# 2x2 average pooling: two result buffers in loop bodies of two tiles, and the wait for the last stores in a section of its own

## Chip, cores, metric

One core of a Trainium2 chip. The metric is the device time of one execution in microseconds (us), as the median of repeated runs.

## The reference

```python
x: (32, 128, 256, 256) float32, kernel_size 2, stride 2
for i in range(128):
    for j in range(128):
        window = x[:, :, 2*i:2*i+2, 2*j:2*j+2]
        output[:, :, i, j] = np.mean(window, axis=(2, 3))
```

1073.7 MB are read and 268.4 MB written; each output is the mean of four inputs.

## The kernel before

Two input rows lie side by side in memory and make one output row, so the work is 524288 rows of 512 floats in and 128 out. A tile is 32 such rows on each of 128 partitions: a load of 8.4 MB (64 KB per partition) and a store of 2.1 MB (16 KB per partition). 127 whole tiles are followed by one that is split into parts of 16, 8, 4 and 4 rows. SyncE (SP) issues loads into two input buffers, VectorE (DVE) adds twice, ScalarE (ACT) scales by 0.25 and issues the store. All waits are written by hand; `take` waits for a semaphore and takes the count off again.

```python
OUTS = 4                                   # result buffers
def tile_sum(b, o, first=False):           # DVE
    it, dst = ins[b], res[o]
    take(dve, loaded[b], 16)
    dve.tensor_add(out=it[:, :, 0:w], in0=it[:, :, 0:w], in1=it[:, :, w:]).then_inc(ready)
    if not first:
        take(dve, stored[o], 16)           # result buffer is free: ahead of the SECOND add
    take(dve, ready)
    dve.tensor_add(out=dst, in0=it[:, :, 0:w:2], in1=it[:, :, 1:w:2]).then_inc(summed)
def tile_scale(b, o, done):                # ACT
    take(act, summed)
    act.sem_inc(free[b])                   # SP may load this input buffer again
    act.mul(out=res[o], in_=res[o], mul=0.25).then_inc(done)
def tile_store(t, o):
    take(act, scaled)
    act.dma_start(out=ot[t], in_=res[o]).then_inc(stored[o], 16)
...                                        # loop bodies of four tiles on DVE and ACT, two on SP
with tc.tile_critical():
    ...
    take(sp, tail, 16 * len(parts))        # the end: four waits, in the one critical section
    for o in range(OUTS):
        if o != whole % OUTS:
            take(sp, stored[o], 16)
```

Of the kernel before, what the change touches and what calls it, by code (L numbers as in the profile page):

```python
# [9 lines left out]
@with_exitstack  # L10
def kernel(
    ctx: ExitStack,
    tc: tile.TileContext,
    x: bass.AP,
    kernel_size: bass.AP,
    stride: bass.AP,
    out: bass.AP,
):
    nc = tc.nc
    P = nc.NUM_PARTITIONS  # L20

    n, c, h, w = x.shape
    k = int(kernel_size)
    s = int(stride)
    h_out = (h - k) // s + 1
    w_out = (w - k) // s + 1
    R = n * c * h_out
    units = R // P if R % P == 0 else 0


    if k == 2 and s == 2 and h % 2 == 0 and w == 256 and units >= 1024:
        _pool_2x2(ctx, tc, x, out, units)
    else:
        _generic_pool(ctx, tc, x, out, k, s, n, c, h, w, h_out, w_out)


TILE = 32
OUTS = 4


def _pool_2x2(ctx, tc, x, out, units):
    nc = tc.nc
    P = nc.NUM_PARTITIONS
    f32 = mybir.dt.float32
    w = x.shape[3]
    w_out = w // 2
    sp, act, dve = nc.sync, nc.scalar, nc.vector

    xv = x.rearrange("n c (ho a) w -> (n c ho) (a w)", a=2)
    ov = out.rearrange("n c ho wo -> (n c ho) wo")  # L50

    in_pool = ctx.enter_context(tc.tile_pool(name="inp", bufs=2))
    out_pool = ctx.enter_context(tc.tile_pool(name="outp", bufs=OUTS))
    ins = [in_pool.tile([P, TILE, 2 * w], f32, name="in_tile") for _ in range(2)]
    res = [out_pool.tile([P, TILE, w_out], f32, name="res") for _ in range(OUTS)]

    loaded = [ctx.enter_context(nc.semaphore(f"loaded{b}")) for b in range(2)]
    free = [ctx.enter_context(nc.semaphore(f"free{b}")) for b in range(2)]
    summed = ctx.enter_context(nc.semaphore("summed"))
    scaled = ctx.enter_context(nc.semaphore("scaled"))  # L60
    stored = [ctx.enter_context(nc.semaphore(f"stored{b}")) for b in range(OUTS)]
    tail = ctx.enter_context(nc.semaphore("tail"))
    ready = ctx.enter_context(nc.semaphore("ready"))
    held = ctx.enter_context(nc.semaphore("held"))



    def take(engine, sem, n=1):
        engine.wait_ge(sem, n)
        engine.sem_inc(sem, -n)  # L70

    def block(r0, g):
        rows = slice(r0, r0 + g * P)
        return xv[rows].rearrange("(p g) f -> p g f", p=P), ov[rows].rearrange("(p g) f -> p g f", p=P)

    whole, rest = divmod(units - 1, TILE)
    rest += 1
    xt = xv[0:whole * TILE * P].rearrange("(t p g) f -> t p g f", p=P, g=TILE)
    ot = ov[0:whole * TILE * P].rearrange("(t p g) f -> t p g f", p=P, g=TILE)
    loops, left = divmod(whole - OUTS, OUTS)  # L80

    def tile_load(t, b):
        sp.dma_start(out=ins[b], in_=xt[t]).then_inc(loaded[b], 16)

    def tile_sum(b, o, first=False):
        it, dst = ins[b], res[o]
        take(dve, loaded[b], 16)
        dve.tensor_add(out=it[:, :, 0:w], in0=it[:, :, 0:w], in1=it[:, :, w:]).then_inc(ready)  # L88
        if not first:
            take(dve, stored[o], 16)  # L90
        take(dve, ready)
        dve.tensor_add(out=dst, in0=it[:, :, 0:w:2], in1=it[:, :, 1:w:2]).then_inc(summed)  # L92

    def tile_scale(b, o, done):
        take(act, summed)
        act.sem_inc(free[b])
        act.mul(out=res[o], in_=res[o], mul=0.25).then_inc(done)  # L97

    def tile_store(t, o):
        take(act, scaled)  # L100
        act.dma_start(out=ot[t], in_=res[o]).then_inc(stored[o], 16)

    parts, a = [], 0
    while a < rest:
        b = rest if rest - a <= 4 else a + (rest - a) // 2
        parts.append((a, b))
        a = b

    psem = [ctx.enter_context(nc.semaphore(f"part{k}")) for k in range(len(parts))]

    with tc.tile_critical():

        for b in range(2):
            tile_load(b, b)
        with sp.Fori(2, 2 + 2 * ((whole - 2) // 2), 2) as i:
            for b in range(2):
                take(sp, free[b])
                tile_load(i + b, b)
        t = 2 + 2 * ((whole - 2) // 2)
        while t < whole:  # L120
            take(sp, free[t % 2])
            tile_load(t, t % 2)
            t += 1



        take(sp, free[whole % 2])
        it, dst = ins[whole % 2], res[whole % OUTS]
        for (a, b), s in zip(parts, psem):
            sp.dma_start(out=it[:, a:b], in_=block((whole * TILE + a) * P, b - a)[0]).then_inc(s, 16)  # L130
        take(sp, held)
        sp.dma_start(out=ot[whole - 1], in_=res[(whole - 1) % OUTS]).then_inc(stored[(whole - 1) % OUTS], 16)


        for o in range(OUTS):
            tile_sum(o % 2, o, first=True)
        with dve.Fori(0, loops) as i:
            for o in range(OUTS):
                tile_sum(o % 2, o)
        for o in range(left):  # L140
            tile_sum(o % 2, o)
        take(dve, stored[whole % OUTS], 16)
        for (a, b), s in zip(parts, psem):
            take(dve, s, 16)
            dve.tensor_add(out=it[:, a:b, 0:w], in0=it[:, a:b, 0:w], in1=it[:, a:b, w:]).then_inc(ready)  # L145
            take(dve, ready)
            dve.tensor_add(out=dst[:, a:b], in0=it[:, a:b, 0:w:2], in1=it[:, a:b, 1:w:2]).then_inc(summed)  # L147


        for t in range(OUTS):  # L150
            tile_scale(t % 2, t, scaled)
            tile_store(t, t)
        with act.Fori(OUTS, OUTS + loops * OUTS, OUTS) as i:
            for o in range(OUTS):
                tile_scale(o % 2, o, scaled)
                tile_store(i + o, o)
        for t in range(OUTS + loops * OUTS, whole):
            tile_scale(t % 2, t % OUTS, scaled if t < whole - 1 else held)
            if t < whole - 1:
                tile_store(t, t % OUTS)  # L160
        act.sem_inc(free[(whole + 1) % 2], -1)
        for a, b in parts:
            take(act, summed)
            act.mul(out=dst[:, a:b], in_=dst[:, a:b], mul=0.25).then_inc(scaled)  # L164
            take(act, scaled)
            act.dma_start(out=block((whole * TILE + a) * P, b - a)[1], in_=dst[:, a:b]).then_inc(tail, 16)


        take(sp, tail, 16 * len(parts))
        for o in range(OUTS):  # L170
            if o != whole % OUTS:
                take(sp, stored[o], 16)


def _generic_pool(ctx, tc, x, out, k, s, n, c, h, w, h_out, w_out):
# [92 lines left out]
```

## Time and profile before

| what | value | from |
|---|---|---|
| time | 3103.83 us (3103.81 to 3103.89, 3 runs) | result |
| span of the profiled run | 3103.1 us | page, first line |
| DVE, ACT busy | 54%, 15% | page, part 1 |
| DMA engines | full in all 40 slices, 433 GB/s | page, part 2 |
| period of a tile | 24.18 us | timeline |
| issue to landing, median | store 33.9, load 34.6 us | page, part 6 |

The page's lines are printed in the prediction. They are read from the resource that has no time left: the DMA row. The wait lists of the page's engines lead only to the line of `take`, and its chain only to the last activation, not to the transfers.

One more view of before is needed for the end of the program: the instructions of the line that holds `take`, and those of the line that opens the critical section, in the last 3 us (columns: line, engine, operation, count; duration in ns; first and last start in us).

```profile
L70 SPq EVENT_SEMAPHORE  x4: 17/17/17, 3101.8 to 3102.0; - x4
L111 SPq NOP  x1: 13/13/13, 3102.3 to 3102.3; - x1
```

Four waits stand one after another behind the last landing, and then SyncE leaves the section it shares with ACT and DVE.

### The profile page before, as it was taken

The numbers are of one execution on the slowest core, as the hardware profiler recorded it, in microseconds if no ns is written. First come the engines' busy times: TensorE is split into PE (matmuls) and PEld (weight loads), VectorE is DVE, ScalarE is ACT, GpSimd is POOL, SyncE is SP. The second block draws the span as 40 slices with busy tenths as digits, with TensorE's granted clock in tenths as the row PEclk, the third lists the DMA queues.
The fourth block names the chain that finished last, engine by engine and source line by source line (L and its number), as shares of the span: only waits on it lengthen the run. The fifth ranks groups of instructions, "written<-read, shape, count | busy, mean of one in ns | idle before, by whom it ended". The sixth has DMA issues, their size and how long they took to land. (4 is left out here: it accounts for less than half of the span.)

```text
span 3103.1 us, 2444 instructions
## 1 busy us (share of the span) xinstructions
DVE 1679.7 (54%) x262; ACT 464.8 (15%) x132; POOL 0.2 (0%) x4
## 2 busy tenths in 40 slices
DVE  4555555555555555555555555555555555555555
ACT  1111111111111111111111111111111111111111
POOL 0000000000000000000000000000000000000000
DMA  9999999999999999999999999999999999999999
GB/s 415 436 439 426 436 439 426 436 439 426 436 438 426 436 438 426 436 430 435 436 438 426 440 435 426 436 438 427 436 438 426 437 439 425 437 438 426 437 438 401
DMA packets 37730, 1342.21 MB, mean 433 GB/s; under 512 B 4192, under 2 KB 4192, under 8 KB 4576
## 3 DMA queue, kind: packets, MB, share of 16 engines
q1 hardware_dynamic: 19008, 1075.85, 80.1%
q10 hardware_dynamic: 18720, 266.35, 20.0%
q14 instruction: 2, 0.02, 0.0%
HBM read 1073.74 MB, written 268.44 MB: 433 GB/s over the span
## 5 line engine op out<-in xcount | busy, mean ns | idle before, releaser
L88 DVE TENSOR_TENSOR in_tile<-in_tile 128x8192 f32<-128x8192 f32 x127 | 1104.0, 8693 | 1395.9 <-DVEq L70 1395.9
L97 ACT ACTIVATE res<-res 128x4096 f32<-128x4096 f32 x127 | 459.2, 3616 | 2587.2 <-ACTq L70 2587.2
L92 DVE TENSOR_TENSOR res<-in_tile 128x4096 f32<-128x4096 f32 x127 | 562.0, 4425 | 18.6
L145 DVE TENSOR_TENSOR in_tile<-in_tile 128x1024 f32<-128x1024 f32 (+2 forms) x4 | 9.1, 2287 | 1.3 <-DVEq L70 1.3
L97 ACT ACT_TABLE_LOAD x1 | 1.3, 1283 | 36.5 <-ACTq L70 36.5
L164 ACT ACTIVATE res<-res 128x512 f32<-128x512 f32 (+2 forms) x4 | 4.2, 1056 | 8.4 <-ACTq L70 8.4
L147 DVE TENSOR_TENSOR res<-in_tile 128x512 f32<-128x512 f32 (+2 forms) x4 | 4.9, 1225 | 0.6
L249 POOL MEMSET const-bfloat16-1.0<- 128x1 bf16 x1 | 0.1, 101 | 0.0
L249 POOL MEMSET const-uint8-127<- 128x1 uint8 x1 | 0.1, 101 | 0.0
L249 POOL MEMSET const-float32-0.0<- 128x1 f32 x1 | 0.1, 98 | 0.2 <-issue 0.2
L249 POOL MEMSET const-float32-1.0<- 128x1 f32 x1 | 0.1, 98 | 0.0
## 6 DMA issues: line engine op xcount, KB each, us to landing
out_dram<-res ACTq DMA_DIRECT2D x126, 2048.0 KB, 33.9
in_tile<-in_x_dram SPq DMA_DIRECT2D x1, 4096.0 KB, 25.1
in_tile<-in_x_dram SPq DMA_DIRECT2D x1, 2048.0 KB, 30.2
in_tile<-in_x_dram SPq DMA_DIRECT2D x2, 1024.0 KB, 33.2
out_dram<-res SPq DMA_DIRECT2D x1, 2048.0 KB, 13.8
in_tile<-in_x_dram SPq DMA_DIRECT2D x127, 34.6
out_dram<-res ACTq DMA_DIRECT2D x1, 1024.0 KB, 7.4
out_dram<-res ACTq DMA_DIRECT2D x1, 512.0 KB, 5.4
```

What stands on the lines that cost most here:

```text
L88: dve.tensor_add(out=it[:, :, 0:w], in0=it[:, :, 0:w], in1=it[:, :, w:]).then_inc(ready)
L92: dve.tensor_add(out=dst, in0=it[:, :, 0:w:2], in1=it[:, :, 1:w:2]).then_inc(summed)
L97: act.mul(out=res[o], in_=res[o], mul=0.25).then_inc(done)
L145: dve.tensor_add(out=it[:, a:b, 0:w], in0=it[:, a:b, 0:w], in1=it[:, a:b, w:]).then_inc(ready)
L147: dve.tensor_add(out=dst[:, a:b], in0=it[:, a:b, 0:w:2], in1=it[:, a:b, 1:w:2]).then_inc(summed)
L164: act.mul(out=dst[:, a:b], in_=dst[:, a:b], mul=0.25).then_inc(scaled)
L249: nc = _bacc.Bacc("TRN2", target_bir_lowering=False, num_devices=1)
```

## The change

Its intent is a shorter program: loop bodies of two tiles with two result buffers (a third for the split tile), one semaphore for all stores that nobody else waits for, and the wait for it in a second critical section that only SyncE enters. The wait for a free result buffer moves in front of the first add.

```diff
-    res = [... for _ in range(OUTS)]            # 4
+    res = [... for _ in range(3)]               # two in rotation, one for the split tile
-    def tile_sum(b, o, first=False):
-        take(dve, loaded[b], 16)
-        dve.tensor_add(...).then_inc(ready)
-        if not first:
-            take(dve, stored[o], 16)
-        take(dve, ready)
-        dve.tensor_add(...).then_inc(summed)
+    def tile_sums(b):
+        take(dve, stored[b], 16)                # now ahead of the FIRST add
+        take(dve, loaded[b], 16)
+        sums(ins[b], res[b])                    # both adds, with `halfway` between them
+        for b in range(2):
+            dve.sem_inc(stored[b], 16)          # both buffers start as free
-        with dve.Fori(0, loops) as i:           # body of four tiles
+        with dve.Fori(0, whole // 2):           # body of two
...
-        take(sp, tail, 16 * len(parts))
-        for o in range(OUTS):
-            if o != whole % OUTS:
-                take(sp, stored[o], 16)
+    with tc.tile_critical():
+        take(sp, tail, 16 * (len(parts) + 2))
```

More of the change, by code (lines that the diff above doesn't have):

```diff
@@ L37 @@
 TILE = 32
-OUTS = 4
 def _pool_2x2(ctx, tc, x, out, units):
@@ L52, in _pool_2x2, with sem @@
     in_pool = ctx.enter_context(tc.tile_pool(name="inp", bufs=2))
-    out_pool = ctx.enter_context(tc.tile_pool(name="outp", bufs=OUTS))
+    out_pool = ctx.enter_context(tc.tile_pool(name="outp", bufs=3))
     ins = [in_pool.tile([P, TILE, 2 * w], f32, name="in_tile") for _ in range(2)]
-    res = [out_pool.tile([P, TILE, w_out], f32, name="res") for _ in range(OUTS)]
-    loaded = [ctx.enter_context(nc.semaphore(f"loaded{b}")) for b in range(2)]
-    free = [ctx.enter_context(nc.semaphore(f"free{b}")) for b in range(2)]
-    summed = ctx.enter_context(nc.semaphore("summed"))
-    scaled = ctx.enter_context(nc.semaphore("scaled"))
-    stored = [ctx.enter_context(nc.semaphore(f"stored{b}")) for b in range(OUTS)]
-    tail = ctx.enter_context(nc.semaphore("tail"))
-    ready = ctx.enter_context(nc.semaphore("ready"))
-    held = ctx.enter_context(nc.semaphore("held"))
+    res = [out_pool.tile([P, TILE, w_out], f32, name="res") for _ in range(3)]
+    def sem(name):
+        return ctx.enter_context(nc.semaphore(name))
+    loaded, free, stored = [[sem(f"{n}{b}") for b in range(2)] for n in ("loaded", "free", "stored")]
+    halfway, summed, scaled, held, tail = [sem(n) for n in ("halfway", "summed", "scaled", "held", "tail")]
     def take(engine, sem, n=1):
@@ L79, in _pool_2x2 @@
     ot = ov[0:whole * TILE * P].rearrange("(t p g) f -> t p g f", p=P, g=TILE)
-    loops, left = divmod(whole - OUTS, OUTS)
-    def tile_load(t, b):
-        sp.dma_start(out=ins[b], in_=xt[t]).then_inc(loaded[b], 16)
-    def tile_sum(b, o, first=False):
-        it, dst = ins[b], res[o]
-        take(dve, loaded[b], 16)
-        dve.tensor_add(out=it[:, :, 0:w], in0=it[:, :, 0:w], in1=it[:, :, w:]).then_inc(ready)
-        if not first:
-            take(dve, stored[o], 16)
-        take(dve, ready)
-        dve.tensor_add(out=dst, in0=it[:, :, 0:w:2], in1=it[:, :, 1:w:2]).then_inc(summed)
-    def tile_scale(b, o, done):
-        take(act, summed)
-        act.sem_inc(free[b])
-        act.mul(out=res[o], in_=res[o], mul=0.25).then_inc(done)
-    def tile_store(t, o):
-        take(act, scaled)
-        act.dma_start(out=ot[t], in_=res[o]).then_inc(stored[o], 16)
     parts, a = [], 0
@@ L105, in _pool_2x2, with load, sums @@
         b = rest if rest - a <= 4 else a + (rest - a) // 2
-        parts.append((a, b))
+        parts.append((a, b, sem(f"part{len(parts)}")))
         a = b
-    psem = [ctx.enter_context(nc.semaphore(f"part{k}")) for k in range(len(parts))]
+    def load(t, b):
+        sp.dma_start(out=ins[b], in_=xt[t]).then_inc(loaded[b], 16)
+    def sums(it, dst):
+        dve.tensor_add(out=it[:, :, 0:w], in0=it[:, :, 0:w], in1=it[:, :, w:]).then_inc(halfway)
+        take(dve, halfway)
+        dve.tensor_add(out=dst, in0=it[:, :, 0:w:2], in1=it[:, :, 1:w:2]).then_inc(summed)
@@ L111, in _pool_2x2, with scale, scale_store @@
+    def tile_sums(b):
+        take(dve, stored[b], 16)
+        take(dve, loaded[b], 16)
+        sums(ins[b], res[b])
+    def scale(dst, done=scaled):
+        act.mul(out=dst, in_=dst, mul=0.25).then_inc(done)
+    def scale_store(t, b, landed):
+        take(act, summed)
+        act.sem_inc(free[b])
+        scale(res[b])
+        take(act, scaled)
+        act.dma_start(out=ot[t], in_=res[b]).then_inc(landed, 16)
     with tc.tile_critical():
-        for b in range(2):
-            tile_load(b, b)
@@ L115, in _pool_2x2 @@
-        with sp.Fori(2, 2 + 2 * ((whole - 2) // 2), 2) as i:
+        load(0, 0)
+        load(1, 1)
+        pairs = (whole - 2) // 2
+        with sp.Fori(2, 2 + 2 * pairs, 2) as i:
             for b in range(2):
                 take(sp, free[b])
-                tile_load(i + b, b)
-        t = 2 + 2 * ((whole - 2) // 2)
-        while t < whole:
+                load(i + b, b)
+        for t in range(2 + 2 * pairs, whole):
             take(sp, free[t % 2])
-            tile_load(t, t % 2)
-            t += 1
+            load(t, t % 2)
@@ L127, in _pool_2x2 @@
         take(sp, free[whole % 2])
-        it, dst = ins[whole % 2], res[whole % OUTS]
-        for (a, b), s in zip(parts, psem):
-            sp.dma_start(out=it[:, a:b], in_=block((whole * TILE + a) * P, b - a)[0]).then_inc(s, 16)
+        it, dst = ins[whole % 2], res[2]
+        for a, b, part in parts:
+            sp.dma_start(out=it[:, a:b], in_=block((whole * TILE + a) * P, b - a)[0]).then_inc(part, 16)
         take(sp, held)
-        sp.dma_start(out=ot[whole - 1], in_=res[(whole - 1) % OUTS]).then_inc(stored[(whole - 1) % OUTS], 16)
@@ L135, in _pool_2x2 @@
-        for o in range(OUTS):
-            tile_sum(o % 2, o, first=True)
-        with dve.Fori(0, loops) as i:
-            for o in range(OUTS):
-                tile_sum(o % 2, o)
-        for o in range(left):
-            tile_sum(o % 2, o)
-        take(dve, stored[whole % OUTS], 16)
-        for (a, b), s in zip(parts, psem):
-            take(dve, s, 16)
-            dve.tensor_add(out=it[:, a:b, 0:w], in0=it[:, a:b, 0:w], in1=it[:, a:b, w:]).then_inc(ready)
-            take(dve, ready)
-            dve.tensor_add(out=dst[:, a:b], in0=it[:, a:b, 0:w:2], in1=it[:, a:b, 1:w:2]).then_inc(summed)
@@ L150, in _pool_2x2 @@
-        for t in range(OUTS):
-            tile_scale(t % 2, t, scaled)
-            tile_store(t, t)
-        with act.Fori(OUTS, OUTS + loops * OUTS, OUTS) as i:
-            for o in range(OUTS):
-                tile_scale(o % 2, o, scaled)
-                tile_store(i + o, o)
-        for t in range(OUTS + loops * OUTS, whole):
-            tile_scale(t % 2, t % OUTS, scaled if t < whole - 1 else held)
-            if t < whole - 1:
-                tile_store(t, t % OUTS)
-        act.sem_inc(free[(whole + 1) % 2], -1)
@@ L162, in _pool_2x2 @@
-        for a, b in parts:
+        sp.dma_start(out=ot[whole - 1], in_=res[(whole - 1) % 2]).then_inc(tail, 16)
+        for b in range(2):
+            dve.sem_inc(stored[b], 16)
+        with dve.Fori(0, whole // 2):
+            for b in range(2):
+                tile_sums(b)
+        if whole % 2:
+            tile_sums(0)
+        for a, b, part in parts:
+            take(dve, part, 16)
+            sums(it[:, a:b], dst[:, a:b])
+        scale_store(0, 0, stored[0])
+        pairs = (whole - 3) // 2
@@ L163, in _pool_2x2 @@
+        with act.Fori(1, 1 + 2 * pairs, 2) as i:
+            for b in (1, 0):
+                scale_store(i + 1 - b, b, stored[b])
+        for t in range(1 + 2 * pairs, whole - 1):
+            scale_store(t, t % 2, stored[t % 2] if t < whole - 2 else tail)
+        take(act, summed)
+        scale(res[(whole - 1) % 2], held)
+        for a, b, _ in parts:
             take(act, summed)
-            act.mul(out=dst[:, a:b], in_=dst[:, a:b], mul=0.25).then_inc(scaled)
+            scale(dst[:, a:b])
@@ L165, in _pool_2x2 @@
             take(act, scaled)
             act.dma_start(out=block((whole * TILE + a) * P, b - a)[1], in_=dst[:, a:b]).then_inc(tail, 16)
-        take(sp, tail, 16 * len(parts))
-        for o in range(OUTS):
-            if o != whole % OUTS:
-                take(sp, stored[o], 16)
+    with tc.tile_critical():
+        take(sp, tail, 16 * (len(parts) + 2))
 def _generic_pool(ctx, tc, x, out, k, s, n, c, h, w, h_out, w_out):
```

## The prediction

> **What bounds the kernel now.** I read the page first: span and busy shares, then the DMA rows.
>
> ```profile
> span 3103.1 us, 2444 instructions
> DVE 1679.7 (54%) x262; ACT 464.8 (15%) x132; POOL 0.2 (0%) x4
> DMA  9999999999999999999999999999999999999999
> q1 hardware_dynamic: 19008, 1075.85, 80.1%
> q10 hardware_dynamic: 18720, 266.35, 20.0%
> HBM read 1073.74 MB, written 268.44 MB: 433 GB/s over the span
> ```
>
> DVE works 54% of the span and ACT 15%, so neither sets it. Loads (q1) and stores (q10) together take 100.1% of the time of the 16 DMA engines. The bytes are fixed by the problem: 1342.2 MB. So the transfers bound the kernel, and a change of buffers and semaphores can only matter where it leaves an engine without work. The second view is the timeline of one tile in the middle, then the issues with their time to landing.
>
> ```profile
> 1519.59 8.69 DVE L88 TENSOR_TENSOR in_tile<-in_tile 128x8192 f32<-128x8192 f32 x1 [10.93 <-DVEq L70]
> 1528.43 4.42 DVE L92 TENSOR_TENSOR res<-in_tile 128x4096 f32<-128x4096 f32 x1
> 1533.05 3.62 ACT L97 ACTIVATE res<-res 128x4096 f32<-128x4096 f32 x1 [20.57 <-ACTq L70]
> 1536.91 0.34 ACTq L101 DMA_DIRECT2D out_dram<-res  x1
> 1543.77 8.69 DVE L88 TENSOR_TENSOR in_tile<-in_tile 128x8192 f32<-128x8192 f32 x1 [10.92 <-DVEq L70]
> ```
> ```profile
> out_dram<-res ACTq DMA_DIRECT2D x126, 2048.0 KB, 33.9
> in_tile<-in_x_dram SPq DMA_DIRECT2D x127, 34.6
> ```
>
> A tile starts every 1543.77 - 1519.59 = 24.18 us. Of these DVE idles 10.9 us for the load. From the first add to the store's issue a tile needs 1536.91 - 1519.59 = 17.3 us, and the store lands 33.9 us later. Third, the tail, by the stretches of the last 36 us (columns: stretch, DVE, ACT, POOL busy, clock, DMA share and GB/s):
>
> ```profile
> 3084.00:3092.00 8.00, 7.71 (x4) 2.17 (x2) 0.00 (x0) 1.00 1.01 427
> 3092.00:3099.00 7.00, 3.82 (x5) 2.31 (x3) 0.00 (x0) 1.00 0.97 405
> 3099.00:3103.00 4.00, 0.00 (x0) 0.00 (x0) 0.00 (x0) 1.00 0.12 45
> ```
>
> The engines are full until 3099. In the packet records behind this view one engine runs about 1.8 us behind the other fifteen. It alone works on after 3099, packet behind packet, to 3101.5. The last store's semaphore is full at 3101.8, SyncE passes its first end wait at 3101.83, and the program ends at 3103.1. The short chain of waits on the page (ACT, 0%) says nothing of this, because it doesn't follow the last DMA.
>
> **What the Trainium skill says.** "DMA: Bandwidth & Descriptors", section Bandwidth, puts the fabric ceiling at 435.2 GB/s. The trace agrees: 433 over the span and 436 to 437 in stretches of one tile. The same page, Queues, rings and completion order, says that each engine goes round-robin between the queues that have work, by packets. The records agree: in the steady state a load packet of 64 KB (2.42 us) and a store packet of 16 KB (0.61 us) alternate, eight of each per tile and engine, 8 x 3.03 = 24.2 us, which is the period. The page's Anatomy of one DMA says that DMA engines do not wait on semaphores; a wait sits in front of the issue. So a late wait costs nothing while the queues hold work. "Runtime: NRT & Kernel Launch", Instruction fetch mechanics, warns that a taken branch can break the prefetch of instructions. No wait of that kind shows in this trace: 2 packets on the instruction queue, and the loops run inside idle time.
>
> **The change, part by part.**
>
> Four result buffers become two in rotation, plus a third for the split last tile, and DVE now waits for the store before its first add instead of its second. This is the part that can cost. Tile t+2 needs the store of tile t landed. Counted from a tile's first add, that store lands at 17.3 + 33.9 = 51.2 us; the load of t+2 lets DVE begin at 2 x 24.18 = 48.4 us. So at the old issue times every sum starts 51.2 - 48.4, about 2.9 us, later than its load would allow, where before (four buffers) there were over 48 us to spare. It takes that out of 10.9 us of idle.
>
> Does the delay come back each round? If the 33.9 us were a fixed latency, the cycle of one buffer would be 51.2 us per two tiles, 25.6 per tile, 1.4 too much. I hold that it is mostly queueing. In the landing records a store (tile 61's, issued 1536.91) finds its predecessor, issued 24.2 us earlier, still in flight for 10 us, 1512.72 + 33.9 = 1546.6. A store issued 2.9 us later only waits 2.9 us less and lands at the same moment. The same holds for the load: issued after the sums at 1533.2, it sits behind its predecessor (issued 1509.02, landed 1543.6) for 10.4 us. After the change 7.5 us are left. For the store 10 - 2.9 = 7 us are left, some 2 less on the fifteen faster engines. Both queues still hold work when the next transfer joins, so no engine runs dry and the period remains 24.18 us. Cost in the 125 middle tiles: 0 us. It is there from the start: the first store lands at 71.6 and the third sum began at 68.7.
>
> The tail. The last full sum starts at most 2.9 us late; the landing records (its load at 3067.0, the store it needs at 3068.9) make it 1.8. DVE ended it with 1.3 us to spare before the first part landed, so the part chain shifts by 1.8 - 1.3 = 0.5 us, 1.8 at the most. The late engine has a backlog then: its last eight packets began at 3100.84, 3.9 us after their issue at 3096.97, while a first packet appears 1.0 us after an issue into empty queues (load 0: issued 0.96, first packet 1.98). Up to 2.9 us of shift are absorbed; cost 0 to 0.3 us.
>
> The end. Before, SyncE made four waits after the last landing (3101.83 to 3102.05), then met ACT and DVE at the end of the critical section (to about 3102.39). After, one wait stands there, and that meeting falls into the 4.8 us in which the last store is in flight, since the first section no longer waits for it. The second section brings one entry (before the landing) and one exit of SyncE alone. I take off three waits at some 0.07 us, 0.2 us, and allow 0.1 for the shorter meeting: -0.3 us.
>
> The start and the bodies. Bodies of two tiles instead of four double the loop branches on DVE and ACT, inside at least 8 us of idle per tile. Two increments that mark the buffers as free stand before the first load lands at 23 us. Fewer semaphores and a shorter program show nowhere on the path. Arithmetic is the same: 127 x (8.69 + 4.42) on DVE, 127 x 3.62 on ACT.
>
> Sum: 3103.83 + 0 (middle) + 0.1 (tail) - 0.3 (end) = 3103.6 us.
>
> **The rivals.** First, the store's landing takes the place of the load's as a real bound. If latency doesn't shrink with a later issue, 1.4 us per tile over 125 tiles, 175 us, time about 3280 us (5.7% slower). For it: 33.9 us is far over the 2 MB's own share of the engines, 8 x 0.61 = 4.9 us, and the wait does change hands. Against it: then all engines would idle 6% of the time, which would empty the queues that make up most of the 33.9 us; the first profile's short queues near the end already show landings of 22.6 and 13.8 us. Second, a partial version: the store queue on the fast engines runs out for one packet, a second load packet slips in, stores land 2.4 us later, and the shift grows until loads too come late. Since an engine with either queue filled keeps working, I expect bubbles of tenths of a us per tile at most; 0.1 us x 125 would make 3116 us. Third, a gain: nothing of the 99% filled span can be saved, so what the end can give is the 1.3 us after the last landing and no more. Even all of it would make 3102.5.
>
> **Range and chances.** The middle estimate is 3103.6. Downward there is only the end, so the range begins at 3102.8. Upward I leave room for the tail's full shift of 1.8 us and for a slip or two at the start: 3106.5. The 2% line lies at 3166, reached only if the first rival holds in large part: 0.03. Faster by 2% is excluded by the bytes: 0.005.
>
> **What would show it.** In the changed profile: the DMA row full of nines and a mid-span period of 24.18 us (step one); DVE's first adds now released by the store, with idle of about 10.9 us per tile as before, each starting about 2.9 us after the load's landing; median store landing down from 33.9 to about 31 us and load landing from 34.6 to about 31.7 (queueing, not latency); last activation at 3096 to 3098 with the last landing still near 3101.8; from there to the end 1.0 instead of 1.3 us. I am wrong if the landings stay at 34 us and the period grows, if DMA slices fall below nine, or if the tail moves one for one with DVE.

## The result

The changed kernel took 3103.45 us (median of 6 runs, 3103.26 to 3104.45) against 3103.94 for the kernel before in the same rounds (3103.81 to 3104.12, 6 runs). The ratio is 0.9999 with a 95% interval of 0.9986 to 1.0012: the same. All outputs were correct.

The page of the changed kernel, the lines that answer to those of before:

```profile
span 3101.8 us, 2621 instructions
...
DVE 1679.5 (54%) x262; ACT 464.7 (15%) x132; POOL 0.2 (0%) x4
...
DMA  9999999999999999999999999999999999999999
...
q1 hardware_dynamic: 19008, 1075.85, 80.1%
q10 hardware_dynamic: 18720, 266.35, 20.1%
```

Busy times, packets and the full DMA row are those of before. The span is 1.3 us shorter, but that is a comparison of two single runs, and the section after next shows why it overstates. The timeline of a tile in the middle, and the issues with their median time to landing:

```profile
1521.24 8.69 DVE L87 TENSOR_TENSOR in_tile<-in_tile 128x8192 f32<-128x8192 f32 x1 [10.94 <-DVEq L67]
1530.08 4.42 DVE L89 TENSOR_TENSOR res<-in_tile 128x4096 f32<-128x4096 f32 x1
1534.69 3.62 ACT L97 ACTIVATE res<-res 128x4096 f32<-128x4096 f32 x1 [20.58 <-ACTq L67]
1538.54 0.34 ACTq L104 DMA_DIRECT2D out_dram<-res  x1
1545.43 8.69 DVE L87 TENSOR_TENSOR in_tile<-in_tile 128x8192 f32<-128x8192 f32 x1 [10.93 <-DVEq L67]
```
```profile
out_dram<-res ACTq DMA_DIRECT2D x126, 2048.0 KB, 30.8
in_tile<-in_x_dram SPq DMA_DIRECT2D x127, 31.5
```

The period is 1545.43 - 1521.24 = 24.19 us as before, and DVE idles as long, 10.9 us. Only the landings have changed: both are 3.1 us shorter. In the landing records the load for the add at 1545.43 was complete on all engines at 1542.16, 3.3 us earlier; the store that it needs was complete at 1545.18, 0.25 us before the add. In the middle (tiles 5 to 125) it is so for every tile: the store is 0.25 us ahead of the add, the load 3.0 to 3.3. So the new wait really is the last to end, and no cost shows in the period.

The end of the program, from the same views as before (L67 is `take`, L157 the second section):

```profile
L67 SPq EVENT_SEMAPHORE  x1: 17/17/17, 3100.8 to 3100.8; - x1
```
```profile
L157 SPq NOP  x2: 13/13/13, 3097.0 to 3101.0; - x2
```

One wait is left. The meeting with ACT and DVE was over, and the second section entered, at 3097.0, while the last store was in flight. By the instruction records, from SyncE's first wait behind the last landing to the end of the program it was 1.24 us before (3101.83 to 3103.07) and is 0.96 us now (3100.81 to 3101.77).

The tail, in the stretches shown of before:

```profile
3084.00:3092.00 8.00, 7.71 (x5) 3.18 (x3) 0.00 (x0) 1.00 1.00 426
3092.00:3099.00 7.00, 3.19 (x4) 1.97 (x3) 0.00 (x0) 1.00 0.98 408
3099.00:3103.00 4.00, 0.00 (x0) 0.00 (x0) 0.00 (x0) 1.00 0.06 23
```

The engines again are full until 3099; the one that works on alone has half as much left (0.06 of 4 us instead of 0.12).

### The profile page after: what moved, and what is told of

The parts are those of the page before. It is cut to its first block, busy times and chain, and to the rows that moved or that the text cites. A ratio compares the mean times of both kernels' runs of the same rounds, so it can differ in the third digit from the quotient of the medians.

```text
span 3101.8 us, 2621 instructions
## 1 busy us (share of the span) xinstructions
DVE 1679.5 (54%) x262; ACT 464.7 (15%) x132; POOL 0.2 (0%) x4
## 3 DMA queue, kind: packets, MB, share of 16 engines
q1 hardware_dynamic: 19008, 1075.85, 80.1%
## 5 line engine op out<-in xcount | busy, mean ns | idle before, releaser
L87 DVE TENSOR_TENSOR in_tile<-in_tile 128x8192 f32<-128x8192 f32 (+1 forms) x131 | 1113.0, 8496 | 1396.7 <-DVEq L67 1396.7
L97 ACT ACTIVATE res<-res 128x4096 f32<-128x4096 f32 (+1 forms) x131 | 463.5, 3538 | 2594.9 <-ACTq L67 2594.9
L89 DVE TENSOR_TENSOR res<-in_tile 128x4096 f32<-128x4096 f32 (+1 forms) x131 | 566.9, 4327 | 19.2
## 6 DMA issues: line engine op xcount, KB each, us to landing
out_dram<-res ACTq DMA_DIRECT2D x126, 2048.0 KB, 30.8
in_tile<-in_x_dram SPq DMA_DIRECT2D x127, 31.5
```

Source lines behind the costliest of these rows:

```text
L97: act.mul(out=dst, in_=dst, mul=0.25).then_inc(done)
```

## The experiments

Theory A at the outset: the transfers bound the kernel, the shorter landings are queueing that gave way to the later issue, and the end saves 0.3 us. Its rivals: a cost of the two buffers hidden behind a larger saving, noise alone, a fixed latency or a least latency of a store. Twelve kernels ran; all gave correct results.

### The parts alone

The changed kernel once more, with no edit:

> The changed kernel itself, unaltered, as the yardstick for the three runs beside it. Theory A (the transfers bound the kernel, the saving is the shorter end alone): 0.3 us below the kernel before, near 3103.5 us. Theory B (the gain of 0.5 us seen so far is noise of one late DMA engine): the medians differ by under 0.1 us, and the single runs of both spread over about 1 us.

Measured: 3103.50 us (3102.68 to 3103.58, 5 runs) against 3104.07 for before (3103.91 to 3104.94, 9 runs), ratio 0.9997. A difference of half a us repeats, and all five runs here lie below all nine of before; but the single runs of each kernel spread over about 1 us, and the interval (0.9984 to 1.0011) holds 1.

Part of that spread has a visible source. In the landing records of the two kernels fifteen engines finish a transfer within about 1 us, and one comes later, by a lag that differs from run to run: half way through, 1.8 us in the profiled run of before, 0.5 in that of the changed kernel, 2.0 in that of b1_long_bodies below. Their last landings are at 3101.8, 3100.8 and 3102.0. The profiled run of before, at 3104.85 us, was one of the late runs, and 1.0 of the 1.3 us between the two spans is the later last landing; that the lag makes it is likely, not shown: in e3_old_end below the lag is 1.3 us and the last landing 3100.8. What sets the lag in a run is open.

The end alone, with four buffers:

```diff
+    tile_store(t, t % OUTS, tail)               # the last stores on `tail`
-        take(sp, tail, 16 * len(parts)); for o ...: take(sp, stored[o], 16)
+    with tc.tile_critical():
+        take(sp, tail, 16 * (len(parts) + OUTS - 1))
```

> The kernel before with its four result buffers and bodies of four tiles, but with the last stores on one semaphore and the wait for it in a second section of SyncE. Theory A: the whole saving of 0.3 us is here, so 3103.5 us against 3103.8; from the last landing to the program's end 0.96 us instead of 1.24. Theory C (a cost of the two buffers, 0.1 to 0.5 us in the tail, is hidden in the changed kernel by a larger saving elsewhere): this run is faster than the changed kernel by 0.1 to 0.5 us, about 3103.2 us.

Measured: 3103.74 us (3103.58 to 3104.15) against the same 3104.07, 0.33 less; from the wait to the end 0.96 us. Not faster than the changed kernel, so a hidden cost of the two buffers does not show. The traces put 1.24 - 0.96 = 0.28 us of the 0.33 at the end.

The buffers and bodies alone, with the old end:

```diff
-    with tc.tile_critical():
-        take(sp, tail, 16 * (len(parts) + 2))
+        take(sp, tail, 16 * len(parts))
+        for b in range(2):
+            take(sp, stored[b], 16)             # the last two stores count on `stored` again
```

> The changed kernel (two result buffers, bodies of two tiles) with the end of the kernel before: one section, and three waits of SyncE after the last landing. Theory A: as slow as the kernel before, 3103.8 us, as the two buffers cost nothing; last landing to end 1.2 us. Theory C: slower than the kernel before by the hidden cost, 3103.9 to 3104.3 us.

Measured: 3103.66 us (3103.43 to 3103.82), with 1.18 us from the first wait to the end. Theory C, which had this run slower than before, finds no support: no cost of the two buffers shows. Theory A fits the order (0.16 us slower than the changed kernel, where the traces give 1.18 - 0.96 = 0.22), but not the level: this run should have been as slow as before and was 0.41 us faster, of which the one wait fewer explains 0.06. The rest, some 0.3 us, is as large as the run-to-run spread of the late engine, and I leave it open. The intervals (0.9985 to 1.0012 here) separate none of these runs; what is firm is the 0.28 us in the traces.

### Is the shorter landing queueing?

The wait goes back between the adds, the two buffers stay:

```diff
-        take(dve, stored[b], 16)
         take(dve, loaded[b], 16)
         dve.tensor_add(...).then_inc(halfway)
+        take(dve, stored[b], 16)
         take(dve, halfway)
```

> The changed kernel with the wait for the store moved back between the two adds, still with two result buffers. The store then lands about 5.8 us before it is needed. Theory A: every first add starts with its load again (about 3 us earlier), median landings go back up to about 33.9 us (store) and 34.6 us (load) because the transfers join a longer queue, and the time stays at 3103.5 us within 0.2. If the 31 us of the changed kernel were due to anything but the later issue, the landings would stay near 31 us here; if the later start cost something, this run would be faster.

Measured: 3103.59 us (3103.39 to 3103.70). The median landings:

```profile
out_dram<-res ACTq DMA_DIRECT2D x126, 2048.0 KB, 34.0
in_tile<-in_x_dram SPq DMA_DIRECT2D x127, 34.6
```

With the adds starting 3 us earlier, both landings are back at the old values and the time is the same. A transfer issued 3 us later lands at the same moment: the 3 us are queueing. A fixed latency is out for this range. The run was needed, because the shorter landing of the changed kernel is no evidence of its own: where a sum waits for the store of two tiles before, 17.3 us to the store's issue, its landing and 0.25 us to the add make up two periods, and 17.3 + 30.8 + 0.25 = 48.4 us, twice 24.2. There the unchanged period is the evidence; in e4 the store is complete 5.9 us before the add that needs it, and the landing can take what value it will.

### How far does it reach?

If an engine keeps working as long as either queue holds something, still later stores should be free too. One, two and four more activations (times 1.0) delay each store's issue:

```diff
         scale(res[b])
+        for _ in range(1):                      # 2 and 4 in the next two runs
+            take(act, scaled)
+            act.mul(out=res[b], in_=res[b], mul=1.0).then_inc(scaled)
         take(act, scaled)
         act.dma_start(...)
```

> The changed kernel with one more activation (times 1.0, the result stays right) of 3.6 us between scaling and store, so each full tile's store is issued about 3.8 us later. Theory A (queueing, an engine works while either queue holds something): no cost, 3103.5 us within 2; the store's landing falls to about 27 us. Rival 1 (31 us is a fixed latency): half of 3.8 us per tile over 125 tiles, about +235 us. Rival 2 (a store amid loads needs at least 28.1 us, as the first store of the changed kernel took): the cycle of a buffer is 17.3 + 3.8 + 28.1 = 49.2 us per two tiles instead of 48.4, +0.4 us per tile, about +50 us.

> Two more activations, the store issued about 7.5 us later. Theory A: by working out when both queues would be empty, still no cost (below +10 us): the loads, let run ahead by the later sums, leave the engine to the stores alone for a time, so the landing shrinks to about 23.5 us. Rival 1: about +470 us. Rival 2: (17.3 + 7.5 + 28.1 - 48.4) / 2 = 2.3 us per tile, about +280 us.

> Four more activations, the store issued about 15 us later, ACT busy 18 of 24.2 us per tile. Theory A is near its limit here, worked out at about 17 us of delay: no cost or a small one, 0 to +60 us, landing about 16 us. Rival 1: about +940 us. Rival 2: (17.3 + 15 + 28.1 - 48.4) / 2 = 6 us per tile, about +750 us.

Measured (2 runs each, before at 3103.83): 3256.19, 3434.34 and 3407.78 us, 152, 331 and 304 us more, ratios 1.049, 1.107 and 1.098. All three theories fail on the sizes. Theory A said free and it was not; a fixed latency said 235, 470, 940; a least latency of 28.1 us said 50, 280, 750. The timeline of the first of them shows what happens instead (some of its lines):

```profile
1496.62 8.69 DVE L87 TENSOR_TENSOR in_tile<-in_tile 128x8192 f32<-128x8192 f32 x1 [20.80 <-DVEq L67]
1513.61 8.69 DVE L87 TENSOR_TENSOR in_tile<-in_tile 128x8192 f32<-128x8192 f32 x1 [3.73 <-DVEq L67]
1517.65 0.34 ACTq L107 DMA_DIRECT2D out_dram<-res  x1
1534.64 0.34 ACTq L107 DMA_DIRECT2D out_dram<-res  x1
1547.55 8.69 DVE L87 TENSOR_TENSOR in_tile<-in_tile 128x8192 f32<-128x8192 f32 x1 [20.68 <-DVEq L67]
1564.54 8.69 DVE L87 TENSOR_TENSOR in_tile<-in_tile 128x8192 f32<-128x8192 f32 x1 [3.72 <-DVEq L67]
```

The even rhythm is gone. Tiles come in pairs, 17.0 us apart and then 33.9, two tiles in 50.93 us or 25.5 each. In the packet records of this stretch no load packet starts between 1508.6 and 1510.6 (40 store packets do), then the engines are empty for part of the next 2 us until a load issued at 1510.2 arrives, and from 1512.6 to 1520.6 loads run alone. First one queue is empty, then the other, and at the turns both. The page puts the loss in two places:

```profile
span 3255.6 us, 2873 instructions
...
DMA  9999999999999999999999999999999999999999
...
q1 hardware_dynamic: 19008, 1075.85, 79.5%
q10 hardware_dynamic: 18720, 266.35, 19.1%
```

Loads and stores now fill 98.6% of the engines' time: 1.4% of 3255.6, some 45 us, is idle. And the same loads take longer: 79.5% of 3255.6 is 2588 us per engine, against 80.1% of 3101.8 = 2485 in the changed kernel, 103 us more. Together that is 148 of the 154 us between the spans. So the DMA row reads nine in every slice while 5% is lost. The packet records say where the loads are slow. Over 50 pairs, 64 KB packets that start in the 2 us after the gap take 3082 ns on average, those that then run alone 2489, those of the next 14 us beside stores 2641, and only the rest the usual 2418.

With two and four activations the tiles run in closer pairs, with no idle between their sums, and the pair takes about 53.5 and 53.2 us. That is why the third is no worse than the second; there the store's landing does shrink, to 15.2 us. With two, most of the loss is idle: the page has 75.2% for loads and 18.1% for stores, so 6.7% of 3433.0 us, 230 us, are empty, and the loads take 97 us longer.

One result buffer for all whole tiles:

```diff
+    res[1] = res[0]                             # and stored[1] becomes stored[0]
```

> The changed kernel with one result buffer for all full tiles (the second name points to the first), so a sum waits for the store of the tile just before it. Theory A: now no queue can hide it, since sums, scaling and store of successive tiles stand in a row: 17.3 us to the issue, then 4 to 6 us of load ahead and store and next load sharing the engines until both are done, about 39 us per tile, near 4950 us, with the DMA row down to some 60%. Rival 1 (fixed 31 us): 17.3 + 31 = 48.3 us per tile, near 6130 us.

Measured: 5304.69 us, ratio 1.71. A tile takes 41.6 us, and 17.3 + 23.9 us of landing is 41.2. Theory A's 4950 is 7% low, fixed latency's 6130 is 16% high; the structure (sums, scaling and store in a row) is as expected, and so is the DMA share, 62% where some 60% were expected.

### Where is the edge, and what makes it one?

A half dose:

```diff
         scale(res[b])
+        take(act, scaled)
+        act.mul(out=res[b][:, :TILE // 2], in_=res[b][:, :TILE // 2], mul=1.0).then_inc(scaled)
```

> The changed kernel with one more activation on half a tile, so each full tile's store is issued about 2.1 us later; 3.8 us cost 152 us. Theory D: the margin that the changed kernel has left is what its store queue still holds when the next store joins, some 2 to 3 us by the records (previous landing less issue 6.6 us, less the 3 to 4 us between an issue and its first packet amid loads), so just no cost yet, 3103.5 us within 2, landing near 28.7 us. If the margin were already used up by the change, about half of the 152 us, 3180 us.

Measured: 3103.76 us (3103.18 to 3104.69, 4 runs) against 3103.84, ratio 1.0001. Free, with the landings down by another 2 us, as two unchanged periods demand (17.3 + 2.1 + 28.8 + 0.25 = 48.4):

```profile
out_dram<-res ACTq DMA_DIRECT2D x126, 2048.0 KB, 28.8
in_tile<-in_x_dram SPq DMA_DIRECT2D x127, 29.3
```

So the edge lies between 2.1 and 3.8 us of further delay. And the dose of two activations, which cost 331 us, with the wait between the adds (the edits of e4 and d2 together):

> Two result buffers, the wait for the store between the two adds, and the stores issued about 7.5 us later by two more activations: the dose that cost 331 us where the wait stood before the first add. Theory D (the loss comes only from the chain late landing, late first add, late load issue, load queue empty, tiles in pairs): between the adds the store has 8.8 us more, so first adds start with their loads, loads are issued on time, and the time is 3103.5 us within 2. Theory E (late stores themselves make the transfers slower, by unmixed queues and longer load packets, wherever the wait stands): most of the 331 us remain, over 3300 us.

Measured: 3106.09 us (3104.13 to 3106.29, 4 runs) against 3103.84, ratio 1.0005. Of the 331 us, 2 remain. Theory E is out: late stores by themselves do not slow the transfers, nor do the added activations. Theory D holds in its main point but not in detail, as two lines of the timeline show:

```profile
1517.27 8.69 DVE L87 TENSOR_TENSOR in_tile<-in_tile 128x8192 f32<-128x8192 f32 x1 [7.57 <-DVEq L67]
1529.48 4.42 DVE L91 TENSOR_TENSOR res<-in_tile 128x4096 f32<-128x4096 f32 x1 [3.52 <-DVEq L67]
```

The second add does wait, 3.5 us. The store lands 60.4 us after the start of its tile's first add, where it landed 51.3 us after it in e4; queueing alone would have kept the 51.3. It has missed its turn, by 9.1 us. So the load is issued 3.5 us late here, and with a landing of 31.3 us against a period of 24.2 it still joins 7.1 us before its predecessor is done. I read d1 from this: there the slip comes on top of the 3 us that the changed kernel already waits, and ahead of both adds, so all of it goes into the load's issue, until the load queue runs empty and the rhythm breaks into pairs. The empty queue and the pairs are in the trace; the size of the slip in d1 is not measured by itself.

An estimate of the edge fits all these runs, but none tests it. A first packet began 3.6 us (first store of d1) and 4.8 us (first store of the kernel before) after an issue beside running loads. A load that joins its queue earlier than that before its predecessor is done finds the queue still at work: 10.4 us in the kernel before, 7.3 in the changed one, 7.1 here, 5.1 with the half dose, all free. The dose of d1 would leave 7.3 - 3.8 = 3.5 us.

### Bodies and packets

Long bodies (four tiles for loads and stores, six for sums):

```diff
-        with dve.Fori(0, whole // 2):
-            for b in range(2): tile_sums(b)
+        with dve.Fori(0, whole // 6):
+            for b in range(6): tile_sums(b % 2)
```

> The changed kernel with loop bodies of four tiles on the load and scale side and six on the sum side, all else equal. The branches stand inside 10 us of idle per tile, so no difference from the changed kernel, 3103.5 us within 0.2. If the short bodies cost something (a stall of instruction fetch at each branch), this run is faster, by 31 or more branches at whatever one costs.

Measured: 3103.42 us (3103.19 to 3104.71, 4 runs) against 3103.94: the changed kernel's time. Short bodies cost nothing that can be seen; the single runs of both kernels spread over more than the 0.2 us foreseen.

Last, an attempt to beat both kernels, with one store of 4 MB for two tiles:

```diff
-    res = [out_pool.tile([P, TILE, w_out], ...) for _ in range(3)]
+    res = [out_pool.tile([P, 2 * TILE, w_out], ...) for _ in range(2)]
+    # tile h of a pair fills res[o][:, h*32:(h+1)*32]; the store follows the second
```

> Two tiles share one result buffer of 32 KB per partition and one store of 4 MB, so a store packet is 32 KB instead of 16 KB; everything else follows the changed kernel. From the packet records a 16 KB packet takes 611 ns and a 32 KB packet 1213 ns, so two small ones cost 9 ns more than a large one: 8 packet pairs per engine and two tiles, 63 times, 4.5 us in all. If the kernel is bound by the packets' own time alone, 3103.5 - 4.5 = 3099 us. If the bursts of stores leave engines idle or lengthen the tail, the gain is eaten up or turns into a loss of some us.

Measured: 3164.52 us (3143.92 to 3187.99, 6 runs), ratio 1.020 (1.017 to 1.024): slower than before, though by the 2% line the verdict is unclear.

```profile
span 3155.3 us, 2207 instructions
...
q1 hardware_dynamic: 19008, 1075.85, 80.4%
q10 hardware_dynamic: 9648, 266.34, 19.6%
```

The store packets gave what was expected: by the packet records they take 611.9 us per engine instead of 615.9. But loads take 80.4% of 3155.3 = 2537 us instead of 2485. There is next to no idle time (80.4 + 19.6 = 100.0%, where the changed kernel has 100.2); the 64 KB load packets average 2472 ns instead of 2420, and in the stretch looked at the long ones (up to 3.25 us) stand at the turn where a burst of stores sets in after a stretch of loads alone. The same lengthening makes up most of d1's loss. Why it happens is not settled.

## Why the prediction was right

The time, 3103.45, lies 0.15 us from the predicted 3103.6 and inside the range. That closeness is partly luck, as single runs spread by 1 us; what was right is the mechanism, no cost per tile and a shorter end. By its steps:

- **What bounds it.** Right. In the middle the change moved only idle time of DVE, and the period stayed at 24.19 us. One reading of the prediction is off: the 436 to 437 GB/s of single stretches, above the ceiling that it cites, come from a view with a DMA share of 1.01; a tile's 10.49 MB in 24.18 us are 433.7.
- **The first sum of each tile about 2.9 us later.** Right: 3.3 us behind the load's landing, where 0.14 us was usual, and the landings shrank to 30.8 and 31.5 (31 and 31.7 foreseen). e4 shows the cause by undoing it.
- **The tail, +0.1.** Not resolvable. The timeline shows DVE going from the last full sums into the parts without the 1.3 us of slack, as foreseen. The last activation started at 3095.6, just outside the 3096 to 3098 foreseen, and the last landing was at 3100.8 instead of 3101.8, probably because the late engine lagged less in this run. The prediction took that lag, read in a single run, for a property of the kernel.
- **The end, -0.3.** Right: 1.24 to 0.96 us in the traces.
- **Bodies and start, 0.** Right by b1.
- **The first rival (fixed latency).** Rightly set at 3%; e4 and f2 refute it for delays up to about 5 us against the kernel before (3.1 + 2.1), as their periods stayed.
- **The second rival, mis-sized.** The prediction put a slipped queue at "tenths of a us per tile at most", since an engine with either queue filled keeps working. d1 measured 152 / 125 = 1.2 us per tile, and two thirds of it with engines that were working, on load packets that took longer. The mechanism was named, but the size was wrong by several times, and so was the distance to it. The changed kernel is 2.1 to 3.8 us of store delay away from losing 5%.
- **What else moved.** The medians differ by about 0.5 us where 0.2 net was foreseen (+0.1 and -0.3); e3 leaves some 0.3 us of that without an explained cause.

## What to carry to other kernels

Where transfers fill the whole span, as here, a landing time can be mostly queue, and a transfer issued a few us later landed at the same moment; landing minus period (load 10.4 us before, 7.3 after, 5.1 with the half dose) is the margin, and not all of it can be used. So "no change in time" may mean that a reserve was spent: measure it by adding delay on purpose. And put a wait for a free output buffer as late as the code allows, here between the two adds, where the dose that cost 331 us cost 2.

## What the Trainium skill lacked or had wrong

- "DMA: Bandwidth & Descriptors", section Bandwidth: its warning that for HBM to SBUF transfers the HBM side at about 358 GB/s binds misleads when read alone, since it takes another note of the section to limit that figure to two cores that stream at once; these kernels, on one core, moved 433 GB/s between HBM and SBUF over the whole span, close to the section's own figure of 425 for one large load. The section also lacks that load packets of one size do not always take the same time: 64 KB in 2420 ns on average here, 2472 with large stores, 2523 with one more activation, 2607 with one buffer.
- The same page, section Latency and other measured facts, gives some 600 ns to the first byte for transfers issued from sync and scalar, and doesn't say from which moment. Here a first packet began 1.0 us after the start of its issue into empty queues, 0.63 us after that instruction's end (0.96, 0.39 long, first packet 1.98), so the figure fits if it counts from the end. It says nothing of an issue beside running transfers: 4.8 us from the start, where loads of 64 KB packets were already running (first store of the kernel before: issued at 41.53, first packet at 46.3).
- No page says how much queue must be left when the next transfer is issued. Here load landings 5.1 us above the period (29.3 - 24.2, the half dose) were still free, and 1.7 us more delay of the store cost 152 us.
